# Gate, up and mixer projections that move a fully normalised activation of 384 columns in place of 386 columns with the shift appended

## The chip, the cores and the metric

The kernel runs on one core of a Trainium2 chip, in one launch. The metric is the device time of the whole program in microseconds: the median of several runs. A profile of one execution gives the trace from which all rows below are taken.

## The reference

One inference step through four layers, on 384 tokens (128 context tokens, group 0, and 256 latent tokens, group 1) of width 1024. Layers 0 and 3 mix tokens by latent attention, layer 1 by a gated linear recurrence over eight heads, layer 2 by windowed attention; each layer ends in a SwiGLU FFN of width 2816. Ahead of each mixer and FFN the activation is normalised and modulated, with a scale and a shift that differ by token group:

```python
def _modulate(x, g, shift, scale):
    return _rmsnorm(x, g) * (1.0 + scale) + shift

def _swiglu(h, w_gate, w_up, w_down):
    return (jax.nn.silu(h @ w_gate) * (h @ w_up)) @ w_down

# the recurrent mixer's projections, each 1024 -> 1024
q = heads(jax.nn.silu(xn @ w_q), HG_DK)
v = heads(xn @ w_i, HG_DV)
f_fwd = lb_fwd + (1.0 - lb_fwd) * jax.nn.sigmoid((xn @ w_f[0]).astype(F32))
f_bwd = lb_bwd + (1.0 - lb_bwd) * jax.nn.sigmoid((xn @ w_f[1]).astype(F32))
g = jax.nn.silu((xn @ w_g).reshape(B, S, HG_HEADS, HG_DV).astype(F32))

# per layer
x = x + g1 * mixer(_modulate(x, norm_mix[i], sh1, sc1))
x = x + g2 * _swiglu(_modulate(x, norm_ffn[i], sh2, sc2), ffn_w_gate[i], ffn_w_up[i], ffn_w_down[i])
```

## The kernel before

The activation lies transposed in SBUF as `xT`, eight chunks of 128 features by 384 tokens. A product with a weight is done in blocks of 128 output features. For each block SP loads 128x1024 numbers into one of four `raw` buffers, ACT rounds them into `whi` (L139), and DVE takes the remainder into `wlo` (L140); there are three buffers of each. The activation is split in the same way into `hh` and `hl`. A block is then 24 matmuls, three for each of eight chunks: hi by hi (L146), hi by lo (L147), lo by hi (L148), all added up in one PSUM bank.

The class `Norm` prepares the activation without waiting for the sum of squares. As each residual chunk is written, `chunk` scales it by `A` (gain times one plus scale) into `hh` and `hl`, and adds up its squares. `shift` writes the two shift vectors (one per token group) into two more columns, 384 and 385, of each chunk. `done` reduces the squares with a matmul on PE (L160), takes the reciprocal root on ACT and DVE (`rst`, `rsy`, `rh`: L163 to L167). `proj` runs a block over 386 columns; the last two columns of its result are the projected shift, copied by DVE into `hb` (L361). `scaled` multiplies the other 384 by `rh` into `ev` (L366). The users add `hb` per token group, in two pieces of 128 and 256 tokens: the Silu on ACT and the product on DVE in the FFN, Sigmoid and products in the recurrent mixer. So the first blocks can run while `rh` is still being made.

In an FFN, gate and up blocks alternate, 22 of each; a gate block uses a PSUM tile `acc` (two buffers), an up block `scps` (three). The product is split into `oh`/`ol` (first eight chunks) and `ah`/`al` for the down projection. In the recurrent layer 40 blocks are projected, four pairs of heads by five kinds, in between the steps of the recurrence of the pair before.

Besides, DVE makes the modulation vectors of coming layers: for one in some weight splits it runs two passes named `apr` over a 128x1024 tile (L274). The order on each engine is set by the tile scheduler that builds the program; each engine runs its instructions strictly in that order.

Of the kernel before, what the change touches and what calls it, by code (L numbers as in the profile page):

```python
# [75 lines left out]
def _build(nc, tc, ia, oa, layers, top):  # L76
# [236 lines left out]
    class Norm:  # L313
        def __init__(self, L, which, split=False):
            need(L, 3 * which + 1)
            self.L, self.which = L, which
            self.A = tp.tile([P, 8, 2], F32, tag="modA", name="modA")
            if not split:
                self.scale(0, 8)
            self.hh = hp.tile([P, KD, TB], F32R, tag="hh", name="hh")  # L320
            self.hl = hp.tile([P, KD, TB], F32R, tag="hl", name="hl")
            self.ss = SumSq("x", KD)

        def scale(self, k0, k1):
            L, which = self.L, self.which
# [19 lines left out]
        def done(self):  # L345
            self.r = rstd_of(self.ss.parts, 1024, tp.tile([P, T], F32, tag="rh", name="rh", bufs=1))

        def proj(self, src, pool, mid=None):
            if early:
                ps, b = early.pop(0)  # L350
                return self.scaled(ps), b
            w = wsplit(src, 1024)
            ps = pool()
            if mid:
                gemm(ps[:, :TB], w, 4, self.hh, self.hl, stop=False)
                mid()
# [493 lines left out]
    def hgrn(L, H):  # L850
        with ExitStack() as es:
# [12 lines left out]
            def head_proj(hpair, i, e, D):  # L864
                h = 2 * hpair + e
                if e == 0:
# [7 lines left out]
                    elif i == 4:  # L874
                        D["v"] = p1.tile([P, 3, 256], F32, tag="v", name="hv")
                t, hb = H.proj(ia["hw"][i, h], acc)
                if ev:
                    dst, tv = ev.pop(0)
                    to_tokens(dst, tv, ttp)
                if i == 4:  # L880
                    addb(V, t, t, hb)
                    ev[0] = (D["v"][:, :, e * 128:(e + 1) * 128], t)
                    return
                sg = p2.tile([P, T], F32, tag="sg", name="sg", bufs=1)
                for vv, c0, c1 in GROUPS:
                    last_silu[0] = S.activation(out=sg[:, c0:c1], in_=t[:, c0:c1], func=AF.Sigmoid,
                                                bias=hb[:, vv:vv + 1])
                if i in (0, 3):
                    for vv, c0, c1 in GROUPS:
                        V.scalar_tensor_tensor(out=D["q" if i == 0 else "g"][:, e, c0:c1], in0=t[:, c0:c1],  # L890
                                               scalar=hb[:, vv:vv + 1], in1=sg[:, c0:c1],
                                               op0=ALU.add, op1=ALU.mult)
# [170 lines left out]
    def ffn(L, H, make_next):  # L1063
        with ExitStack() as es:
# [5 lines left out]
            al = p1.tile([P, NFF - KD, T], F32R, name="al")  # L1070
            for f in range(NFF):
                tg, bg = H.proj(ia["gu"][L, f, 0], acc)
                tu, bu = H.proj(ia["gu"][L, f, 1], scp)
                s = p2.tile([P, T], F32, tag="s", name="s")
                for v, c0, c1 in GROUPS:
                    last_silu[0] = S.activation(out=s[:, c0:c1], in_=tg[:, c0:c1], func=AF.Silu, bias=bg[:, v:v + 1])
                for v, c0, c1 in GROUPS:
                    V.scalar_tensor_tensor(out=s[:, c0:c1], in0=tu[:, c0:c1], scalar=bu[:, v:v + 1],
                                           in1=s[:, c0:c1], op0=ALU.add, op1=ALU.mult)
# [241 lines left out]
```

## Time and profile before

| | |
|---|---|
| three runs | 1935.99, 1936.65, 1937.23 us (median 1936.65) |
| profiled execution | 1938.45 us, span of its instructions 1936.7 us |
| granted TensorE clock, mean | 0.996 of full speed |
| PE busy | 1899.5 us, 98 % |
| PEld (weight loads) busy | 1812.3 us, 94 % |
| DVE busy | 1556.3 us, 80 % |
| ACT busy | 873.5 us, 45 % |
| POOL busy | 44.4 us, 2 % |
| DMA | 313.44 MB, mean 162 GB/s |

Busy time counts each stretch in which at least one instruction of the engine is under way. Matmuls are pipelined: each lasts longer than the step from its start to the next one's, so a busy PE says that it never stood still, not how fast it went.

### The profile page before, as it was taken

The numbers are of one execution on the slowest core, as the hardware profiler recorded it, in microseconds if no ns is written. First come the engines' busy times: TensorE is split into PE (matmuls) and PEld (weight loads), VectorE is DVE, ScalarE is ACT, GpSimd is POOL, SyncE is SP. The second block draws the span as 40 slices with busy tenths as digits, with TensorE's granted clock in tenths as the row PEclk, the third lists the DMA queues.
The fourth block names the chain that finished last, engine by engine and source line by source line (L and its number), as shares of the span: only waits on it lengthen the run. The fifth ranks groups of instructions, "written<-read, shape, count | busy, mean of one in ns | idle before, by whom it ended". The sixth has DMA issues, their size and how long they took to land.

```text
span 1936.7 us, 29416 instructions
## 1 busy us (share of the span) xinstructions
PE 1899.5 (98%) x10939; PEld 1812.3 (94%) x10939; DVE 1556.3 (80%) x3097; ACT 873.5 (45%) x1622; POOL 44.4 (2%) x52
## 2 busy tenths in 40 slices
PE   8999999999999999999999999999999999999997
PEld 5768999999999999999999878999999889999997
DVE  3867898888999999898878988989878897755533
ACT  4534534333554554433433675443434555433332
POOL 0000000000011100000000100000000000000000
PEclk9999999999999999999999999999999999999999
DMA  8553566667533334566667423666667334443342
GB/s 331 169 158 112 183 190 208 201 196 207 167 109 100 109 99 125 189 193 207 194 202 228 132 63 123 211 202 199 195 209 213 107 104 142 131 127 124 119 126 71
DMA packets 99343, 313.44 MB, mean 162 GB/s; under 512 B 11008, under 2 KB 20736, under 8 KB 99200
## 3 DMA queue, kind: packets, MB, share of 16 engines
q1 hardware_dynamic: 98768, 310.78, 51.0%
q8 instruction: 86, 1.41, 0.3%
q10 hardware_dynamic: 432, 0.79, 0.1%
q14 instruction: 57, 0.47, 0.1%
HBM read 305.95 MB, written 3.21 MB: 160 GB/s over the span
## 4 chain that ended last, share of the span: by engine, by line
PE 93%; DVE 3%; DMA 2%; ACT 1%; issue 1%; SPq 0%; DVEq 0%; ACTq 0%
PE acc L146 16%; PE acc L147 16%; PE acc L148 16%; PE scps L146 11%; PE scps L147 11%; PE scps L148 11%; PE scps L916 2%; PE misps L506 2%; PE ttps L245 1%; DMA araw<-ada 1%; PE ttps L495 1%; PE ttps L226 1%; DVE apr L274 1%; PE ttps L499 1%; PE misps L160 1%
## 5 line engine op out<-in xcount | busy, mean ns | idle before, releaser
L139 ACT ACTIVATE whi<-raw 128x1024 fp32r<-128x1024 f32 (+1 forms) x381 | 396.6, 1042 | 687.9 <-PE acc L147 327.2
L140 DVE TENSOR_TENSOR wlo<-raw,whi 128x1024 fp32r<-128x1024 f32 x380 | 455.9, 1201 | 109.2 <-ACT whi L139 105.4
L146 PE MATMUL acc<-hh,whi 128*128 128x386 f32 (+1 forms) x1160 | 398.6, 344 | 0.0
L147 PE MATMUL acc<-hl,whi 128*128 128x386 f32 (+1 forms) x1160 | 395.8, 341 | 0.0
L148 PE MATMUL acc<-hh,wlo 128*128 128x386 f32 (+1 forms) x1160 | 393.5, 339 | 0.0
L274 DVE SCALAR_TENSOR_TENSOR apr<-araw,cbc 128x1024 f32<-128x1024 f32 x320 | 390.2, 1219 | 1.8
L146 PE MATMUL scps<-hh,whi 128*128 128x386 f32 (+1 forms) x776 | 264.7, 341 | 0.8 <-ACT hh L341 0.8
L147 PE MATMUL scps<-hl,whi 128*128 128x386 f32 (+1 forms) x776 | 263.5, 340 | 0.3
L148 PE MATMUL scps<-hh,wlo 128*128 128x386 f32 (+1 forms) x776 | 262.4, 338 | 0.0
L146 PEld LDWEIGHTS acc<-hh,whi 128*128 128x128 f32 x1160 | 218.9, 189 | 2.0 <-issue 1.8
L147 PEld LDWEIGHTS acc<-hl,whi 128*128 128x128 f32 x1160 | 219.7, 189 | 0.9
L148 PEld LDWEIGHTS acc<-hh,wlo 128*128 128x128 f32 x1160 | 218.8, 189 | 1.6 <-issue 0.4
L146 PEld LDWEIGHTS scps<-hh,whi 128*128 128x128 f32 x776 | 146.2, 188 | 5.2 <-issue 1.7
L147 PEld LDWEIGHTS scps<-hl,whi 128*128 128x128 f32 x776 | 147.0, 189 | 1.4 <-DVE hl L342 1.1
L148 PEld LDWEIGHTS scps<-hh,wlo 128*128 128x128 f32 x776 | 146.4, 189 | 0.8 <-issue 0.8
L146 PE MATMUL acc<-oh,whi 128*128 128x384 f32 x344 | 118.6, 347 | 7.4 <-DVE xT L387 1.9
L147 PE MATMUL acc<-ol,whi 128*128 128x384 f32 x344 | 118.0, 343 | 0.0
L148 PE MATMUL acc<-oh,wlo 128*128 128x384 f32 x344 | 117.7, 342 | 0.0
L366 DVE TENSOR_TENSOR ev<-acc,rh 128x384 f32<-128x384 f32 x145 | 79.5, 548 | 0.1
L146 PEld LDWEIGHTS acc<-oh,whi 128*128 128x128 f32 x344 | 64.8, 190 | 11.4 <-issue 5.2
L146 PE MATMUL scps<-ah,whi 128*128 128x384 f32 x224 | 75.3, 336 | 0.0
L146 PE MATMUL acc<-ah,whi 128*128 128x384 f32 x224 | 75.3, 336 | 0.0
(309 smaller groups left out, 3196.1 us busy)
## 6 DMA issues: line engine op xcount, KB each, us to landing
raw<-gu SPq DMA_DIRECT2D x176, 512.0 KB, 4.1
araw<-adaT SPq DMA_DIRECT2D x160, 512.0 KB, 3.7
raw<-dn SPq DMA_DIRECT2D x64, 512.0 KB, 4.1
raw<-hw SPq DMA_DIRECT2D x40, 512.0 KB, 3.7
raw<-dn SPq DMA_DIRECT2D x32, 384.0 KB, 3.2
stg<-ada SPq DMA_DIRECT2D x16, 512.0 KB, 6.6
araw<-ada SPq DMA_DIRECT2D x16, 512.0 KB, 4.2
raw<-mo SPq DMA_DIRECT2D x16, 512.0 KB, 3.8
```

The costliest lines, as they stand in the source:

```text
L139: a = S.activation(out=hi[:, :cols], in_=raw[:, :cols], func=AF.Copy)
L140: b = eng.tensor_tensor(out=lo[:, :cols], in0=raw[:, :cols], in1=hi[:, :cols].bitcast(F32), op=ALU.subtract)
L146: TE.matmul(out, lhsT=ah, rhs=bh, start=start, stop=False)
L147: TE.matmul(out, lhsT=ah, rhs=bl, start=False, stop=False)
L148: TE.matmul(out, lhsT=al, rhs=bh, start=False, stop=stop)
L160: TE.matmul(ps, lhsT=ones[n], rhs=q, start=i == 0, stop=i == len(sumsq) - 1)
L226: TE.matmul(ps[32 * q:32 * q + 32, :], lhsT=cond[:, k, :], rhs=raw[:, k2 * 512:(k2 + 1) * 512], start=k < 4, stop=k >= 4, tile_position=(0 ...
L245: TE.matmul(ps[32 * ct:32 * ct + 32, :], lhsT=cond[:, k, :], rhs=raw[:, c2 * 512:(c2 + 1) * 512], start=k == 0, stop=k == 7, tile_position ...
L274: V.scalar_tensor_tensor(out=pr, in0=raw, scalar=1.0, in1=cbc[:, v], op0=ALU.mult, op1=ALU.mult, accum_out=mod_of(L)[:, seg, k, v:v + 1])
L366: V.tensor_tensor(out=t, in0=ps[:, :T], in1=self.r, op=ALU.mult)
L506: TE.matmul(out[:, 128:384], lhsT=v[:, 1 + j, c0:c1], rhs=pt[:, 128 + 256 * j:384 + 256 * j], start=j == 0, stop=j == 2, **kw)
L916: TE.matmul(ps[:, tt], lhsT=Lt[:, e, tt], rhs=rhs(e, t), start=True, stop=True)
```

## The change

In FFNs and in the recurrent mixer the first block runs as before, over 386 columns. The next three run side by side (`group`): for each chunk, three matmuls of each of the three blocks into three PSUM tiles, and then that chunk is rewritten in place by `whole`: `xT` times `rh` on DVE (`hx`), scale and shift on ACT in two pieces, rounding into `hh` on ACT, remainder into `hl` on DVE. All later blocks read 384 columns of the rewritten chunks, and their result is used straight from PSUM, without `hb` and `ev`. The third weight of a group is split into a spare tile: `ah`/`al` in the FFN, which is not in use yet. Attention mixers keep the old form.

```diff
+        def whole(self, k):
+            h = tp.tile([P, T], F32, tag="sq", name="hx")
+            B = mods[self.L][:, 3 * self.which, k]
+            V.tensor_tensor(out=h, in0=xT[:, k], in1=self.r, op=ALU.mult)
+            for v, c0, c1 in GROUPS:
+                S.activation(out=h[:, c0:c1], in_=h[:, c0:c1], func=AF.Identity, scale=self.A[:, k, v:v + 1],
+                             bias=B[:, v:v + 1])
+            S.activation(out=self.hh[:, k, 0:T], in_=h, func=AF.Copy)
+            V.tensor_tensor(out=self.hl[:, k, 0:T], in0=h, in1=self.hh[:, k, 0:T].bitcast(F32), op=ALU.subtract)
+
+        def group(self, blocks):
+            ws = [wsplit(src, 1024, into=into) for src, _, into in blocks]
+            pss = [pool() for _, pool, _ in blocks]
+            for k in range(KD):
+                for (hi, lo), ps in zip(ws, pss):
+                    c = slice(k * 128, k * 128 + 128)
+                    mm3(ps[:, :TB], hi[:, c], lo[:, c], self.hh[:, k], self.hl[:, k], k == 0, k == KD - 1)
+                self.whole(k)
+            self.begun.extend(pss)
+            self.full = True
+
         def proj(self, src, pool, mid=None):
...
+            if self.begun:
+                ps = self.begun.pop(0)
+                b = tp.tile([P, 2], F32, tag="hb", name="hb", bufs=8)
+                V.tensor_copy(out=b, in_=ps[:, T:TB])
+                return self.scaled(ps), b
             w = wsplit(src, 1024)
             ps = pool()
+            if self.full:
+                gemm(ps[:, :T], w, 8, self.hh[:, :, 0:T], self.hl[:, :, 0:T])
+                return ps[:, :T], None
...
                 t, hb = H.proj(ia["hw"][i, h], acc)
+                if not H.full:
+                    H.group([(ia["hw"][1, h + 1], scp, None), (ia["hw"][2, h], acc, None),
+                             (ia["hw"][2, h + 1], scp, spare2())])
...
                 tg, bg = H.proj(ia["gu"][L, f, 0], acc)
+                if f == 0:
+                    spare = [x.rearrange("p f t -> p (f t)")[:, 0:1024] for x in (ah, al)]
+                    H.group([(ia["gu"][L, 0, 1], scp, None), (ia["gu"][L, 1, 0], acc, None),
+                             (ia["gu"][L, 1, 1], scp, spare)])
                 tu, bu = H.proj(ia["gu"][L, f, 1], scp)
                 s = p2.tile([P, T], F32, tag="s", name="s")
...
+                if bg is None:
+                    last_silu[0] = S.activation(out=s, in_=tg, func=AF.Silu)
+                    V.tensor_tensor(out=s, in0=tu, in1=s, op=ALU.mult)
```

First place: DVE in layer 0's FFN. Before, where the third to fifth blocks are evicted (numbers tell buffers apart; L361 is the bias copy, L366 the multiplication by `rh`, L1078 the product's halves, L1082 the remainder of the product, L140 a weight split):

```order
L361 COPY hb_2158<-acc_2133 128x2
L366 TENSOR_TENSOR ev_2160<-acc_2133,rh_2026 128x384
L274 SCALAR_TENSOR_TENSOR apr_2212,mod_113<-araw_2089,cbc_93 128x1024
L140 TENSOR_TENSOR wlo_2247<-raw_2244,whi_2246 128x1024
L361 COPY hb_2195<-scps_2170 128x2
L366 TENSOR_TENSOR ev_2197<-scps_2170,rh_2026 128x384
L1078 SCALAR_TENSOR_TENSOR s_2199<-ev_2197,hb_2195,s_2199 128x128
L1078 SCALAR_TENSOR_TENSOR s_2199<-ev_2197,hb_2195,s_2199 128x256
```

After the change, the evictions of the three grouped blocks stand among the rewrites (L353 is `hx`, L358 the new `hl`; L378 and L397 copy the bias and multiply by `rh`). Directly ahead of these rows stand the bias copy and the multiplication of the first grouped block, `scps_2103`, and ahead of those the rewrites of chunks 0 to 2 and the `hx` of chunks 3 and 4:

```order
L378 COPY hb_2237<-acc_2104 128x2
L1121 SCALAR_TENSOR_TENSOR s_2230<-ev_2228,hb_2226,s_2230 128x128
L1121 SCALAR_TENSOR_TENSOR s_2230<-ev_2228,hb_2226,s_2230 128x256
L358 TENSOR_TENSOR hl_1785<-hx_2160,hh_1784 128x384
L397 TENSOR_TENSOR ev_2239<-acc_2104,rh_2026 128x384
L353 TENSOR_TENSOR hx_2190<-xT_78,rh_2026 128x384
L1125 TENSOR_TENSOR ol_2045<-s_2230,oh_2044 128x384
L358 TENSOR_TENSOR hl_1785<-hx_2175,hh_1784 128x384
L378 COPY hb_2241<-scps_2105 128x2
L353 TENSOR_TENSOR hx_2205<-xT_78,rh_2026 128x384
L397 TENSOR_TENSOR ev_2243<-scps_2105,rh_2026 128x384
L140 TENSOR_TENSOR wlo_2289<-raw_2286,whi_2288 128x1024
```

The `hl` of chunks 3 and 4 and the split for the sixth block now stand behind evictions of grouped blocks, which end together.

Second place: PE behind the group in the same FFN. Before, blocks followed each other whole (here the end of the fourth and the start of the fifth; L146 to L148 as above):

```order
L146 MATMUL scps_2170<-hh_1784,whi_2164 128x386
L147 MATMUL scps_2170<-hl_1785,whi_2164 128x386
L148 MATMUL scps_2170<-hh_1784,wlo_2165 128x386
L146 MATMUL acc_2215<-hh_1784,whi_2208 128x386
L147 MATMUL acc_2215<-hl_1785,whi_2208 128x386
L148 MATMUL acc_2215<-hh_1784,wlo_2209 128x386
```

After, the fifth block (`acc_2261`) has done four chunks when the sixth (`scps_2294`) is woven in; the rows are the 13th to the 20th behind the group:

```order
L146 MATMUL acc_2261<-hh_1784,whi_2254 128x384
L146 MATMUL scps_2294<-hh_1784,whi_2288 128x384
L147 MATMUL scps_2294<-hl_1785,whi_2288 128x384
L147 MATMUL acc_2261<-hl_1785,whi_2254 128x384
L148 MATMUL acc_2261<-hh_1784,wlo_2255 128x384
L146 MATMUL acc_2261<-hh_1784,whi_2254 128x384
L148 MATMUL scps_2294<-hh_1784,wlo_2289 128x384
L146 MATMUL scps_2294<-hh_1784,whi_2288 128x384
```

The first matmul that reads `wlo_2289` has 18 matmuls ahead of it since the group's end; the `hl` of the last chunk is read after 39. In layer 1's FFN these counts are 15 and 45, in layer 2's 18 and 46, in layer 3's as in layer 0's; in the recurrent layer the fifth block runs whole, and the last `hl` is read after 22.

Third place: DVE in layer 2's FFN, from the first step of the reciprocal root. Before:

```order
L165 SCALAR_TENSOR_TENSOR rst_12238<-misps_12235,rsy_12237 128x384
L361 COPY hb_12290<-acc_12265 128x2
L166 SCALAR_TENSOR_TENSOR rst_12238<-rst_12238,rsy_12237 128x384
L274 SCALAR_TENSOR_TENSOR apr_12344,mod_8438<-araw_12191,cbc_93 128x1024
L167 SCALAR_TENSOR_TENSOR rh_12234<-rst_12238,rsy_12237 128x384
L274 SCALAR_TENSOR_TENSOR apr_12344,mod_8438<-araw_12191,cbc_93 128x1024
L366 TENSOR_TENSOR ev_12292<-acc_12265,rh_12234 128x384
L361 COPY hb_12327<-scps_12302 128x2
L366 TENSOR_TENSOR ev_12329<-scps_12302,rh_12234 128x384
L140 TENSOR_TENSOR wlo_12381<-raw_12378,whi_12380 128x1024
```

After:

```order
L165 SCALAR_TENSOR_TENSOR rst_11790<-misps_11787,rsy_11789 128x384
L392 COPY hb_11842<-acc_11817 128x2
L166 SCALAR_TENSOR_TENSOR rst_11790<-rst_11790,rsy_11789 128x384
L274 SCALAR_TENSOR_TENSOR apr_11860,mod_8136<-araw_11743,cbc_93 128x1024
L167 SCALAR_TENSOR_TENSOR rh_11786<-rst_11790,rsy_11789 128x384
L274 SCALAR_TENSOR_TENSOR apr_11860,mod_8136<-araw_11743,cbc_93 128x1024
L397 TENSOR_TENSOR ev_11844<-acc_11817,rh_11786 128x384
L140 TENSOR_TENSOR al_11807<-raw_11865,ah_11806 128x1024
L353 TENSOR_TENSOR hx_11881<-xT_78,rh_11786 128x384
L353 TENSOR_TENSOR hx_11896<-xT_78,rh_11786 128x384
L140 TENSOR_TENSOR wlo_12021<-raw_12018,whi_12020 128x1024
L274 SCALAR_TENSOR_TENSOR apr_12024,mod_8136<-araw_11852,cbc_93 128x1024
```

The split of the group's third weight (`al`) now stands behind `rh`, and the first `hl` comes after it, another split and a further `apr`. From the first of these rows to the `hl` of chunk 7 there are 42 in all: 25 of 384 columns, six `apr`, three splits, two pairs of halves and four bias copies. In the recurrent layer the same stretch has 46: 25 of 384 columns, two splits, two `apr`, four bias copies and 13 small ones.

## Rows read from the trace of the kernel before

**Rows 1.** The page, part 1: busy us (share of the span) xinstructions by engine.

```profile
PE 1899.5 (98%) x10939; PEld 1812.3 (94%) x10939; DVE 1556.3 (80%) x3097; ACT 873.5 (45%) x1622; POOL 44.4 (2%) x52
```

**Rows 2.** Busy time by stretch: us, PE, PEld, DVE, ACT, POOL, clock, DMA, GB/s.

```profile
217.00:403.00 186.00, 186.00 (x1055) 185.87 (x1054) 162.94 (x305) 77.22 (x114) 0.00 (x0) 1.00 0.63 194
495.00:782.00 287.00, 282.78 (x1802) 277.10 (x1801) 267.98 (x576) 150.28 (x326) 25.86 (x23) 1.00 0.36 114
```

**Rows 3.** Timeline of PE, matmuls of three widths: start, duration, line, operation.

```profile
222.96 0.34 PE L146 MATMUL acc<-hh,whi 128*128 128x386 f32 x1
...
231.43 0.34 PE L146 MATMUL acc<-hh,whi 128*128 128x386 f32 x1
...
420.12 0.34 PE L146 MATMUL scps<-ah,whi 128*128 128x384 f32 x1
...
423.76 0.33 PE L146 MATMUL acc<-oh,whi 128*128 128x384 f32 x1
...
427.97 0.34 PE L146 MATMUL acc<-ah,whi 128*128 128x384 f32 x1
...
33.68 0.34 PE L147 MATMUL scps<-hl,whi 128*128 128x384 f32 x1
...
35.60 0.34 PE L146 MATMUL scps<-hh,whi 128*128 128x384 f32 x1
...
1518.04 0.39 PE L612 MATMUL acc<-whi,ch 128*128 128x512 f32 x1
...
1519.20 0.40 PE L614 MATMUL acc<-whi,cl 128*128 128x512 f32 x1
```

**Rows 4.** Weight loads by line and form: count, busy us, mean ns, idle before.

```profile
L147 PEld LDWEIGHTS acc<-hl,whi 128*128 128x128 f32 x1160 | 219.7, 189 | 0.9
```

**Rows 5.** Timeline of DVE in layer 0's FFN, 232 to 236 us.

```profile
232.37 0.75 DVE L1078 SCALAR_TENSOR_TENSOR s<-ev,hb,s 128x128 f32<-128x128 f32 x2
233.04 1.22 DVE L140 TENSOR_TENSOR wlo<-raw,whi 128x1024 fp32r<-128x1024 f32 x1
234.17 0.55 DVE L1082 TENSOR_TENSOR ol<-s,oh 128x384 fp32r<-128x384 f32 x1
234.64 1.22 DVE L274 SCALAR_TENSOR_TENSOR apr<-araw,cbc 128x1024 f32<-128x1024 f32 x1
235.79 0.08 DVE L274 DVE_READ_ACCUMULATOR apr<-araw,cbc 128x1 f32 x1
235.86 0.16 DVE L361 COPY hb<-acc 128x2 f32<-128x2 f32 x1
235.94 0.55 DVE L366 TENSOR_TENSOR ev<-acc,rh 128x384 f32<-128x384 f32 x1
```

**Rows 6.** ACT operations by line and form: count, busy us, mean ns, idle before.

```profile
L139 ACT ACTIVATE whi<-raw 128x1024 fp32r<-128x1024 f32 x349 | 369.5, 1060 | 626.6 <-PE acc L147 296.8 <-issue 242.5 <-PE scps L147 85.2
L341 ACT ACTIVATE hh<-xT,modA 128x256 fp32r<-128x256 f32 x64 | 31.7, 496 | 0.0
L1081 ACT ACTIVATE ah<-s 128x384 fp32r<-128x384 f32 x56 | 29.5, 526 | 72.8 <-DVE s L1078 72.8
L341 ACT ACTIVATE hh<-xT,modA 128x128 fp32r<-128x128 f32 x64 | 24.9, 389 | 2.8 <-DVE xT L387 1.6 <-DVE modA L327 1.0
```

**Rows 7.** Timeline of PE: first matmul of the fifth block in layers 1, 2.

```profile
796.29 0.34 PE L146 MATMUL acc<-hh,whi 128*128 128x386 f32 x1
...
1225.62 0.34 PE L146 MATMUL acc<-hh,whi 128*128 128x386 f32 x1
```

**Rows 8.** Timeline of DVE: recurrent layer, and the root in layer 2's FFN.

```profile
497.92 0.55 DVE L165 SCALAR_TENSOR_TENSOR rst<-misps,rsy 128x384 f32<-128x384 f32 x1
...
510.77 0.16 DVE L361 COPY hb<-acc 128x2 f32<-128x2 f32 x1 [0.70 <-PE acc L148]
...
1213.45 0.55 DVE L165 SCALAR_TENSOR_TENSOR rst<-misps,rsy 128x384 f32<-128x384 f32 x1
```

**Rows 9.** Timeline of DVE: a remainder that waits for ACT's rounding.

```profile
337.24 0.56 DVE L1082 TENSOR_TENSOR al<-s,ah 128x384 fp32r<-128x384 f32 x1 [0.29 <-ACT ah L1081]
```

More of the change, by code (lines that the diff above doesn't have):

```diff
@@ L322, in __init__ @@
             self.ss = SumSq("x", KD)
+            self.begun = []
+            self.full = False
         def scale(self, k0, k1):
@@ L880, in head_proj @@
                 if i == 4:
-                    addb(V, t, t, hb)
-                    ev[0] = (D["v"][:, :, e * 128:(e + 1) * 128], t)
+                    tv = tp.tile([P, T], F32, tag="ev", name="ev", bufs=3)
+                    V.tensor_copy(out=tv, in_=t)
+                    ev[0] = (D["v"][:, :, e * 128:(e + 1) * 128], tv)
                     return
                 sg = p2.tile([P, T], F32, tag="sg", name="sg", bufs=1)
-                for vv, c0, c1 in GROUPS:
-                    last_silu[0] = S.activation(out=sg[:, c0:c1], in_=t[:, c0:c1], func=AF.Sigmoid,
-                                                bias=hb[:, vv:vv + 1])
+                if hb is None:
+                    last_silu[0] = S.activation(out=sg, in_=t, func=AF.Sigmoid)
+                else:
+                    for vv, c0, c1 in GROUPS:
+                        last_silu[0] = S.activation(out=sg[:, c0:c1], in_=t[:, c0:c1], func=AF.Sigmoid,
+                                                    bias=hb[:, vv:vv + 1])
                 if i in (0, 3):
[L889 to L892, printed above, removed]
+                    V.tensor_tensor(out=D["q" if i == 0 else "g"][:, e], in0=t, in1=sg, op=ALU.mult)
                 else:
@@ L1072, in ffn @@
                 tg, bg = H.proj(ia["gu"][L, f, 0], acc)
+                if f == 0:
+                    spare = [x.rearrange("p f t -> p (f t)")[:, 0:1024] for x in (ah, al)]
+                    H.group([(ia["gu"][L, 0, 1], scp, None), (ia["gu"][L, 1, 0], acc, None),
+                             (ia["gu"][L, 1, 1], scp, spare)])
                 tu, bu = H.proj(ia["gu"][L, f, 1], scp)
                 s = p2.tile([P, T], F32, tag="s", name="s")
[L1075 to L1079, printed above, removed]
+                if bg is None:
+                    last_silu[0] = S.activation(out=s, in_=tg, func=AF.Silu)
+                    V.tensor_tensor(out=s, in0=tu, in1=s, op=ALU.mult)
+                else:
+                    for v, c0, c1 in GROUPS:
+                        last_silu[0] = S.activation(out=s[:, c0:c1], in_=tg[:, c0:c1], func=AF.Silu, bias=bg[:, v:v + 1])
+                    for v, c0, c1 in GROUPS:
+                        V.scalar_tensor_tensor(out=s[:, c0:c1], in0=tu[:, c0:c1], scalar=bu[:, v:v + 1],
+                                               in1=s[:, c0:c1], op0=ALU.add, op1=ALU.mult)
                 dh, dl = (bh[:, f], bl[:, f]) if f < KD else (ah[:, f - KD], al[:, f - KD])
```

## Prediction

> **What bounds the kernel now.** I read the page's busy shares first: PE has work in flight for 1899.5 of 1936.7 us [rows 1]. Then busy time by stretch. In the 186 us of gate and up blocks of layer 0's FFN, matmuls and weight loads are both solid, DVE is busy 162.9 us and ACT 77.2; the recurrent layer (495 to 782 us) leaves PE idle only 4.2 of 287 us, with DVE busy 268 [rows 2]. So in the stretches that the change touches PE sets the time, and it has no stall to give back. What can move the end is the time from one matmul to the next, and any new wait of PE. DVE is second, at 88 to 93 per cent. For prices I then read the timelines, since the duration of a row is no price: matmuls overlap, and a DVE row starts before the one ahead has ended. Steps from start to start count.
>
> **Narrower matmuls.** By the two listings, 4704 matmuls go from 386 to 384 columns: 40 blocks of 24 in each of four FFNs, 36 of 24 in the recurrent layer. Two whole 386 blocks take 222.96 to 231.43, 48 steps of 176.5 ns. At 384 columns the steps are 173.3 ns from `ah` (21 steps, 420.12 to 423.76), 175.4 from `oh` (24 steps, 423.76 to 427.97), and 174.5 from `hh` itself in the first layer's early blocks (11 steps, 33.68 to 35.60) [rows 3]. That is 1.1 to 3.2 ns less for each. The rows on `hh` are the nearest, but they are few and stand in another stage; between them (2.0) and `oh` (1.1) I take 1.5 ns: 4704 x 1.5 = 7.1 us gained. The bounds are 4.2 us (below) and 4704 x 3.2 = 15 us.
>
> Is the step set by columns at all? 512 columns take 232 ns (five steps, 1518.04 to 1519.20) and 384 some 174, with the same 128x128 weight load of 189 ns in front [rows 3, 4]: 58 ns for 128 columns, 0.45 ns a column, so two columns are worth 0.9 ns, or 4.2 us over all. The Trainium skill ("TensorE: Matmul & The Clock Gate", Back-to-back issue gap) says that in a stream of load and matmul pairs both set the spacing. By it, with loads as solid as they are here, the narrowing could be worth nothing; the 512-column rows speak against that.
>
> **Work that goes.** Of the later blocks, the bias copies, the multiplications by `rh` and one of each pair of halves go from DVE. With the steps of [rows 5] (0.08 for a copy, 0.47 for a 384-wide tensor operation, 0.67 for a pair of halves) that is some 1.3 us of DVE per gate and up pair. It lies beside matmuls throughout: PE has no wait there for it to shorten, so I cost it at nothing. In the recurrent layer it could return part of the 4.2 us of PE idle time; I take zero and keep 4.2 as a bound.
>
> **Work that comes, and where.** Each rewrite of a chunk is two DVE operations of 384 (0.47 each) and on ACT two Identity pieces and a Copy, by the nearest rows 0.39, 0.50 and 0.53 us long [rows 6], about 1.1 us by steps. Eight chunks are 7.5 us of DVE and 9 of ACT. The cover is the group: 72 matmuls, 12.7 us of PE. But chunk k may only be rewritten when the group's three blocks have read it, nothing can start before `rh`, and both engines still have their old work. So I add up what stands on DVE.
>
> *FFN of layer 0.* In the listing, the bias copy of the first grouped block (`hb<-scps`) stands ahead of the `hl` of chunks 3 to 7, so it cannot start until that block's last matmul, seven from the group's end: 231.43 - 7 x 0.1765 + 0.34 = 230.53. From it to the end of the split that the next up block needs (`wlo`) stand three small copies (0.3 with their latency), two halves (0.67), eight operations of 384 (3.8) and the split (1.22): 6.0 us, so 236.5. PE reaches the first matmul on that `wlo` after 18 others, at 231.43 + 18 x 0.175 = 234.6 [rows 3, 5]. PE waits **1.9 us**. The order in layer 3's FFN is the same: **1.9 us**.
>
> *FFN of layer 1.* The same chain of 6.0 us starts 0.86 before the group's end at 796.29 [rows 7]; the `wlo` is wanted after 15 matmuls: 801.4 against 798.9, **2.5 us**.
>
> *FFN of layer 2.* Here the sums for the next layer's modulation (`apr`, 1.22 us a step) lie thickest. From the first `rst` at 1213.45 [rows 8] to the last `hl` DVE has 25 operations of 384 (11.75), six `apr` (7.3), three splits (3.4), two pairs of halves (1.3) and four copies (0.4): 24.3 us with the last one's full length, so 1237.7. PE wants it after 46 matmuls from 1225.62 [rows 7], at 1233.7: **4.1 us**, spread over several chunks.
>
> *Recurrent layer.* The copies of blocks 2 to 4 follow their last matmuls, the third at 510.77 [rows 8]; so the group ends at 510.77 - 0.03 - 0.34 + 0.18 = 510.6. From `rst` at 497.92 DVE has 25 operations of 384 (11.75, the two forget gates taken alike), two splits (2.3), two `apr` (2.4), four copies (0.4) and 13 small ones (1.3): 18.3 us, so 516.2. In this order nothing of another block fills the gap: the last `hl` is wanted after 22 matmuls, at 514.4. That is 1.8 us, and with the next block's split behind it 0.5 more: **2.3 us**.
>
> The five come to 12.7 us. These sums leave out the waits of DVE for ACT and back; one such hand-over shows 0.29 us of idle DVE [rows 9]. At one for each place I add 1.5: 14.2 us. If each of eight chunks paid it in each place, it would be 12 us instead. The lower bound is half the 12.7, since later matmuls of other blocks could use part of each wait.
>
> **Sum.** 14.2 - 7.1 = +7.1 us. The profiled execution took 1938.45 us (span 1936.7), so its like would take 1945.6; the median of the runs is 1.8 us lower than that execution, hence 1936.65 + 7.1 = **1943.8 us**. A difference under 0.2 per cent (3.9 us) can't be told from none.
>
> **Rivals.**
> *The rewriting is hidden, and the kernel is faster.* If PE never meets a late chunk, only the columns count: 1929.6, or 1922 with the 3.2 ns of the `ah` rows. For it: ACT is busy under half of the stretch [rows 2]. Against it: the chain of 6.0 us that starts after the first grouped block has finished, whatever ACT does. It decides when that chain is under some 4 us.
>
> *A draw.* Waits of 7 us and 7 us of columns, or 12.7 against the full 15. Time about 1936.
>
> *Weight loads set the pace.* Nothing from the columns: 1936.65 + 14.2 = 1951. For it: loads without a gap [rows 2]; against it: the steps of [rows 3].
>
> *A wait ahead of the group.* The group's third weight is split early into the spare tile, ahead of the chunks of the last residual on ACT; where its load has not landed, ACT stops, the sum of squares comes late, and the reduction that stands inside block 1 on PE with it. One split is 1.22 on DVE and 1.06 on ACT; if it delays PE once at each of five places it is 5 us more: 1949.
>
> *The narrowing doesn't show.* The chunks of `hh` keep their 386-column stride; if the start of a chunk and not its width makes `hh` slower than `ah` (176.5 against 173.3), the lower bound of 4.2 us holds, and the time is 1946.7; that lies within the forecast's own case.
>
> **Chances.** Waits exceed the columns, by 4 to 13 us: 0.58. Loads set the pace: 0.04. The wait ahead of the group adds its 5 us: 0.05. All three are slower. Draw: 0.20. Hidden and faster: 0.13. So slower 0.67, same 0.20, faster 0.13. Waits between 6.4 and 25 us and columns between 4.2 and 15 give extremes of -9 and +20; leaving out the far ends of both, one in ten on each side, gives 1933 to 1952. The forecast's own case runs from 1940.5 to 1950.
>
> **What the new profile would show.** Right: later gate and up blocks step at about 175 ns, with no bias copies and no multiplications by `rh` between them; PE idle times after each of the five groups, released by DVE (`wlo`, `hl`) or ACT (`hh`), of 2 to 4 us in all, most in layer 2; DVE busy about 137 us (162.9 less 20 pairs of 1.3) in the 186 us of FFN. Wrong: PE solid through the blocks behind the groups; or 386 and 384 columns at one step; or a stall in block 1, ahead of the group. It would be wrong above all if PE's order lets other matmuls run through each wait, or if the steps at 384 columns come out at 173.

## The result, and the profile after the change

| | before | after |
|---|---|---|
| median of the runs | 1936.43 us (1935.99 to 1937.23, 4 runs) | 1950.77 us (1949.61 to 1951.14, 4 runs) |
| ratio, with its 95 % interval | | 1.0074 (1.0061 to 1.0087) |
| span of the profiled execution | 1936.7 us | 1949.3 us |

The change made the kernel 14.3 us slower. The forecast said slower (0.67), 1943.8 us, 1933 to 1952: the side and the range held, the size was half of what came.

The page of the changed kernel, part 1, answers to [rows 1]:

```profile
PE 1906.9 (98%) x10939; PEld 1810.9 (93%) x10939; DVE 1464.5 (75%) x2681; ACT 883.4 (45%) x1634; POOL 44.3 (2%) x52
```

DVE lost 92 us of work and PE gained 7 us of busy time with the same count of matmuls: the work taken off bought nothing in the FFNs, and 1.8 us in the recurrent layer (shown in the part on the prediction). The first view to read is what PE waited for (us in total, times, the longest); before, only the last kind was there, with 0.6 us:

```profile
PE acc L146 <- ACT hh L357: 3.9, 8, 0.6
...
PE scps L148 <- DVE wlo L140: 1.6, 3, 0.5
...
PE acc L147 <- DVE hl L358: 1.2, 5, 0.4
...
PE acc L148 <- DVE wlo L140: 0.8, 2, 0.6
```

They are idle time alone, 7.5 us with the 0.6 of before among them, and less than the loss. The steps from one matmul's start to the next tell more. The table takes each stretch from the first matmul of one reduction (L160) to that of the next. "Waits" is what its steps over 230 ns hold beyond 175 ns, steps of 310 to 330 ns set apart, both less the same in the trace of before; the reduction's own first step is left out.

| stretch | before, us | after, us | difference | waits | steps of 320 ns |
|---|---|---|---|---|---|
| FFN, layer 0 | 278.64 | 279.70 | +1.06 | 2.11 | 0 |
| recurrent layer | 286.98 | 291.43 | +4.45 | 2.72 | 2.16 (15 more) |
| FFN, layer 1 | 278.30 | 280.92 | +2.62 | 3.68 | 0 |
| FFN, layer 2 | 279.52 | 284.85 | +5.33 | 4.31 | 2.03 (14) |
| FFN, layer 3 | 276.18 | 277.25 | +1.07 | 2.12 | 0 |

Waits are 14.9 us and the steps of 320 ns 4.2; the five differences are 14.5, so 4.6 us came back, which wide and norewrite below put down to the columns. (Ahead of the first stretch the changed kernel was 1.6 us earlier in this execution; in the profiles of the kernels that leave that part as it was, the stretch starts anywhere from 215.0 to 216.6 us. The mixers of layers 2 and 3 differ by -0.3 and +0.2.)

In the recurrent layer the last two columns are net figures. Behind the group alone the waits hold 4.8 us, and 13 steps of 320 ns 1.9; in the rest of the layer the two together come to 1.8 less than before. In the FFNs nearly all lies behind the group. So the five groups cost 17.0 us of waits (0.2 of them ahead of layer 2's), and 27 steps of 320 ns 3.9.

**A wait that came as worked out.** Layer 0's FFN, DVE and PE, from the timelines:

```profile
228.98 0.16 DVE L378 COPY hb<-scps 128x2 f32<-128x2 f32 x1 [1.18 <-PE scps L148]
...
233.72 1.21 DVE L140 TENSOR_TENSOR wlo<-raw,whi 128x1024 fp32r<-128x1024 f32 x1
...
234.03 0.44 PE L146 MATMUL acc<-hh,whi 128*128 128x384 f32 x1 [0.61 <-ACT hh L357]
234.99 0.44 PE L148 MATMUL scps<-hh,wlo 128*128 128x384 f32 x1 [0.52 <-DVE wlo L140]
235.26 0.34 PE L146 MATMUL scps<-hh,whi 128*128 128x384 f32 x1
```

The bias copy waits for the first grouped block, and the split that PE needs ends at 234.93. The forecast had 230.53 and 236.5 on the clock of before, 228.96 and 234.93 with the 1.57 us that this stretch began earlier. Each wait also costs more than its idle time: the step behind it is 0.27 to 0.29 us in place of 0.175.

**What was not in the forecast.** In the recurrent layer, PE's busy time (count), granted clock, DMA share and GB/s by stretches of 1 us:

```profile
511.00:512.00 1.00, 1.00 (x8) 1.00 0.25 98
...
513.00:514.00 1.00, 0.55 (x2) 1.00 0.00 0
514.00:515.00 1.00, 0.51 (x2) 1.00 0.00 0
515.00:516.00 1.00, 0.76 (x3) 1.00 0.00 0
516.00:517.00 1.00, 0.64 (x3) 0.91 0.00 0
517.00:518.00 1.00, 0.99 (x3) 0.50 0.00 0
...
522.00:523.00 1.00, 1.00 (x5) 0.50 0.75 131
523.00:524.00 1.00, 1.00 (x6) 0.68 0.51 201
524.00:525.00 1.00, 1.00 (x7) 1.00 0.71 291
```

and PE's timeline there:

```profile
515.09 0.44 PE L146 MATMUL acc<-hh,whi 128*128 128x384 f32 x1 [0.59 <-ACT hh L357]
...
516.67 0.59 PE L146 MATMUL acc<-hh,whi 128*128 128x384 f32 x1 [0.36 <-ACT hh L357]
...
521.05 0.53 PE L147 MATMUL acc<-hl,whi 128*128 128x384 f32 x1
521.37 0.53 PE L148 MATMUL acc<-hh,wlo 128*128 128x384 f32 x1
521.69 0.53 PE L146 MATMUL acc<-hh,whi 128*128 128x384 f32 x1
```

From 513 on PE stands still by turns, never over 0.6 us at a time. At some 517 the granted clock goes from full to 0.50, which is 1.2 GHz, and stays there until 523.7; the last matmul that waits starts at 519.3. In that time a step is 320 ns in place of 175: a matmul that waits for nobody costs 0.145 us more. In layer 2's FFN the same lasts from 1237 to 1244. The Trainium skill ("TensorE: Matmul & The Clock Gate", A second HAM failure mode: psum-queue depth-cycling) tells of short idle times of PE between groups of matmuls that are enough to throttle the clock; the trace agrees.

### The profile page after: what moved, and what is told of

It is laid out like the page before. It is cut to its first block, busy times and chain, and to the rows that moved or that the text cites. A ratio compares the mean times of both kernels' runs of the same rounds, so it can differ in the third digit from the quotient of the medians.

```text
span 1949.3 us, 29058 instructions
## 1 busy us (share of the span) xinstructions
PE 1906.9 (98%) x10939; PEld 1810.9 (93%) x10939; DVE 1464.5 (75%) x2681; ACT 883.4 (45%) x1634; POOL 44.3 (2%) x52
## 4 chain that ended last, share of the span: by engine, by line
PE 91%; DVE 4%; ACT 2%; DMA 2%; issue 1%; SPq 0%; DVEq 0%; ACTq 0%
PE acc L146 16%; PE acc L148 16%; PE acc L147 16%; PE scps L148 11%; PE scps L147 11%; PE scps L146 11%; PE scps L951 2%; PE misps L537 2%; PE ttps L245 1%; DMA araw<-ada 1%; PE ttps L526 1%; PE ttps L226 1%; PE ttps L530 1%; PE misps L160 1%; DVE apr L274 1%
## 5 line engine op out<-in xcount | busy, mean ns | idle before, releaser
L139 ACT ACTIVATE whi<-raw 128x1024 fp32r<-128x1024 f32 (+1 forms) x376 | 391.3, 1042 | 793.6 <-issue 374.8
L140 DVE TENSOR_TENSOR wlo<-raw,whi 128x1024 fp32r<-128x1024 f32 (+1 forms) x375 | 449.4, 1199 | 221.0 <-ACT whi L139 213.5
L146 PE MATMUL acc<-hh,whi 128*128 128x384 f32 (+1 forms) x1144 | 393.6, 344 | 4.1 <-ACT hh L357 3.9
L147 PE MATMUL acc<-hl,whi 128*128 128x384 f32 (+1 forms) x1144 | 392.3, 343 | 1.3 <-DVE hl L358 1.2
L148 PE MATMUL acc<-hh,wlo 128*128 128x384 f32 (+1 forms) x1144 | 390.0, 341 | 0.3 <-DVE wlo L140 0.3
L148 PE MATMUL scps<-hh,wlo 128*128 128x384 f32 (+1 forms) x752 | 255.7, 340 | 1.6 <-DVE wlo L140 1.6
L146 PE MATMUL scps<-hh,whi 128*128 128x384 f32 (+1 forms) x752 | 254.7, 339 | 1.2 <-ACT hh L343 0.8
L147 PE MATMUL scps<-hl,whi 128*128 128x384 f32 (+1 forms) x752 | 255.4, 340 | 0.3
L146 PEld LDWEIGHTS acc<-hh,whi 128*128 128x128 f32 x1144 | 217.1, 190 | 10.9 <-ACT hh L357 8.5
L147 PEld LDWEIGHTS acc<-hl,whi 128*128 128x128 f32 x1144 | 216.3, 189 | 5.1 <-DVE hl L358 4.0
L148 PEld LDWEIGHTS acc<-hh,wlo 128*128 128x128 f32 x1144 | 217.1, 190 | 2.5 <-DVE wlo L140 0.9
L146 PEld LDWEIGHTS scps<-hh,whi 128*128 128x128 f32 x752 | 142.4, 189 | 5.1 <-issue 1.7
L148 PEld LDWEIGHTS scps<-hh,wlo 128*128 128x128 f32 x752 | 142.6, 190 | 3.2 <-DVE wlo L140 2.3
L147 PEld LDWEIGHTS scps<-hl,whi 128*128 128x128 f32 x752 | 141.8, 189 | 1.4 <-DVE hl L344 1.1
L146 PE MATMUL acc<-oh,whi 128*128 128x384 f32 x344 | 118.7, 347 | 5.9 <-DVE xT L418 1.9
L147 PE MATMUL acc<-ol,whi 128*128 128x384 f32 x344 | 117.8, 342 | 0.0
L148 PE MATMUL acc<-oh,wlo 128*128 128x384 f32 x344 | 117.6, 342 | 0.0
L1116 DVE TENSOR_TENSOR s<-scps,s 128x384 f32<-128x384 f32 x80 | 44.4, 555 | 82.2 <-PE scps L148 82.2
L146 PE MATMUL acc<-ah,whi 128*128 128x384 f32 x224 | 75.3, 336 | 0.0
L146 PE MATMUL scps<-ah,whi 128*128 128x384 f32 x224 | 75.3, 336 | 0.0
L147 PE MATMUL acc<-al,whi 128*128 128x384 f32 x224 | 75.3, 336 | 0.0
```

Of the source, the lines that this page charges most:

```text
L139: a = S.activation(out=hi[:, :cols], in_=raw[:, :cols], func=AF.Copy)
L140: b = eng.tensor_tensor(out=lo[:, :cols], in0=raw[:, :cols], in1=hi[:, :cols].bitcast(F32), op=ALU.subtract)
L146: TE.matmul(out, lhsT=ah, rhs=bh, start=start, stop=False)
L147: TE.matmul(out, lhsT=ah, rhs=bl, start=False, stop=False)
L148: TE.matmul(out, lhsT=al, rhs=bh, start=False, stop=stop)
L1116: V.tensor_tensor(out=s, in0=tu, in1=s, op=ALU.mult)
```

## Experiments

Each was timed in five rounds against the kernel before, which stood at 1936.1 to 1936.3 us. All differences below, of a stretch or a median, are to the kernel before unless said otherwise. Differences of whole profiled spans hold one thing that no edit made: in layer 3's mixer the traces of before, of the changed kernel and of pool have 16 to 19 steps of 320 ns, those of all others 5 to 8, three among them, which leaves this mixer as it was. That is 1.2 to 2 us of such a span. By stretch (as in the table above; FFNs by their layer):

| kernel | median, us | FFN 0 | recurrent | FFN 1 | FFN 2 | FFN 3 |
|---|---|---|---|---|---|---|
| changed | 1950.77 | +1.06 | +4.45 | +2.62 | +5.33 | +1.07 |
| wide | 1954.27 | +2.07 | +4.55 | +4.65 | +5.09 | +2.08 |
| fill | 1947.09 | +1.05 | +2.58 | +2.61 | +3.74 | +1.11 |
| three | 1942.17 | +1.10 | -0.03 | +2.61 | +0.00 | +1.09 |
| norewrite | 1931.49 | -1.09 | -0.62 | -1.13 | -0.74 | -1.06 |
| pool | 1962.39 | +5.02 | +6.04 | +4.14 | +6.45 | +6.34 |
| hx8 | 1947.59 | +0.92 | +1.31 | +3.84 | +4.67 | +0.95 |
| hold | 1939.57 | +0.72 | +1.32 | +1.25 | +0.47 | +0.75 |
| hx8_hold | 1936.31 | +0.14 | +0.55 | +0.43 | -0.12 | +0.18 |
| ffn_hx8_hold | 1938.06 | +0.16 | -0.62 | +0.44 | -0.07 | +0.18 |

### What the columns are worth: wide, norewrite

```diff
 wide
-                gemm(ps[:, :T], w, 8, self.hh[:, :, 0:T], self.hl[:, :, 0:T])
+                gemm(ps[:, :TB], w, 8, self.hh, self.hl)
 norewrite
-                self.whole(k)
...
-                return ps[:, :T], None
+                return self.scaled(ps), self.hb
```

> The changed kernel, but the later blocks move all 386 columns again (their last two results are not used). Forecast's price of 1.5 ns for each of 4704 matmuls: 7.1 us slower than the changed kernel, about 1957.9. By the steps in the new trace (24 matmuls of a later FFN block 4.208 us against 4.233, in the recurrent layer 4.291 against 4.305): 160 x 0.026 + 36 x 0.014 = 4.7 us slower, about 1955.5. If width counts for nothing: 1950.8, with steps still at 4.208 us per block.

> The changed kernel without the rewriting: chunks stay as they were, later blocks move 384 columns and are multiplied by rh at their eviction as before; their shift is left out (the first one's stands in for it). Theory that the loss is the rewriting's waits and the clock that falls on them, and that the narrowing gives 26 ns a block in the FFNs and 14 in the recurrent layer: no wait behind the groups, no step of 320 ns there, 1936.4 - 4.7 = 1931.7. By the forecast's 1.5 ns a matmul: 1929.3. If running three blocks side by side or the early third split costs by itself: 1934 or more.

wide: ratio 1.0092 (1.0079 to 1.0106), 3.5 us over the changed kernel by the medians, where 4.7 were expected. In layers 0 and 3, where no clock fell in either, the stretch grew by exactly 1.01 us, 40 blocks of 0.025. The other places mix in a clock that fell in layer 1's FFN (10 steps of 320 ns, none before) and for a shorter time in layer 2's. norewrite: 1931.49, ratio 0.9978 (0.9969 to 0.9987), against 1931.7 expected. PE is solid behind the groups, at full clock, and the FFNs are 0.7 to 1.1 us shorter. So the grouping and the early third split cost next to nothing (0.3 us of waits in layer 2's FFN); the loss is the rewriting, and the most that this narrowing can give by itself is 4.7 us. PE behind the group in the recurrent layer (the columns are PE's busy time, count, granted clock, DMA share and GB/s):

```profile
511.00:517.00 6.00, 6.00 (x36) 1.00 0.71 192
```

The steps themselves, two whole blocks later on in the changed kernel (48 steps of 175.2 ns), and in wide (176.25):

```profile
303.49 0.33 PE L146 MATMUL scps<-hh,whi 128*128 128x384 f32 x1
...
311.90 0.33 PE L146 MATMUL scps<-hh,whi 128*128 128x384 f32 x1
```

```profile
304.31 0.34 PE L146 MATMUL scps<-hh,whi 128*128 128x386 f32 x1
...
312.77 0.34 PE L146 MATMUL scps<-hh,whi 128*128 128x386 f32 x1
```

### Whether the clock fell on PE's standstill: fill, three

```diff
 fill: in the first block behind the group, two places, FILL = (0, 0, 4, 4, 4, 4, 4, 4)
+                    for k in range(KD):
+                        mm3(ps[:, :T], ..., self.hh[:, k, 0:T], self.hl[:, k, 0:T], k == 0, k == KD - 1)
+                        for _ in range(FILL[k]):
+                            TE.matmul(junk[:, :T], lhsT=w[0][:, 0:128], rhs=self.hh[:, 0, 0:T], ...)
 three: the recurrent layer in its old form, and
-                if f == 0:
+                if f == 0 and L != 2:
```

> The changed kernel, with 48 matmuls more, whose results nobody reads, in the fifth block of the recurrent layer and of layer 2's FFN: they read a chunk that is already rewritten, and stand on PE between the chunks that come late. If PE's own standstill is what the clock fell on: no steps of 320 ns in these two places, the granted clock stays at 1.0 there, 4.4 us less than the changed kernel (about 1946.4), or up to 2 us less good where a chunk comes in time and the added matmuls (48 x 0.175 = 8.4 us in all, against some 8 us of waits) hold PE up. If the 320 ns came from DVE and ACT at work on the same memory, which the filling does not change: the steps stay at 320 ns, and the time rises by up to 8 us. If the waits alone made the loss: no gain.

> The change in the FFNs of layers 0, 1 and 3 alone; the recurrent layer and layer 2's FFN as before. Theory that the loss lies in two places (between the reductions, +4.45 us in the recurrent layer and +5.33 in layer 2's FFN): 1950.8 - 9.8 = 1941.0, which is still 4.5 us above the kernel before, with layers 0 and 3 at +1.1 and layer 1 at +2.6, and no step of 320 ns behind a group. Rival: the loss is spread, or it comes from the scheduler's changed order elsewhere: over 1944. If the two places are all of it: 1936.

fill: 1947.09, ratio 1.0058 (1.0045 to 1.0071), 3.7 us under the changed kernel where 4.4 were expected. In the recurrent layer, the same columns as above:

```profile
513.00:514.00 1.00, 1.00 (x8) 1.00 0.03 8
...
516.00:517.00 1.00, 1.00 (x8) 1.00 0.00 0
...
520.00:521.00 1.00, 0.71 (x4) 1.00 0.00 0
521.00:522.00 1.00, 1.00 (x8) 1.00 0.68 70
```

PE does useless work for about as long as it would have waited, DVE and ACT do what they did (8.24 and 9.87 us busy in the ten from 511, against 8.24 and 10.00 in the changed kernel's ten from 510), and the clock stays at full. The 24 added matmuls of each place take 4.2 us; the waits behind the group fell from 4.8 to 0.5 us in the recurrent layer and from 4.3 to 0.5 in layer 2's FFN. The 1.87 and 1.59 us won by place are the half clock less what the filling held up. So PE's own standstill brought the clock down: the work of DVE and ACT on the same memory was the same as before, and the 320 ns are gone.

three: 1942.17, ratio 1.0029 (1.0018 to 1.004), 1941.0 expected. The three stretches that keep the change stand at +1.10, +2.61 and +1.09 and the two others at 0: each place pays for itself.

### Where the waits come from: pool, hx8, hold

```diff
 pool
-            V.tensor_tensor(out=h, in0=xT[:, k], in1=self.r, op=ALU.mult)
+            G.tensor_tensor(out=h, in0=xT[:, k], in1=self.r, op=ALU.mult)
 hx8: a place of its own for each chunk's hx (FFN: al's memory, al itself taken at f == 8)
-            h = tp.tile([P, T], F32, tag="sq", name="hx")
...
-                self.whole(k)
+                self.whole(k, hx[k])
 hold: FEED = 0.66, HOLD = 6
     def ada_tick(d, a, b):
+        if hold[0]:
+            return
...
         def done(self):
+            hold[0] = self.which == 1
...
         def proj(self, src, pool, mid=None):
+            if self.full:
+                self.n += 1
+                if self.n > HOLD:
+                    hold[0] = False
```

> The changed kernel with the first step of a rewrite (hx, xT times rh) on POOL in place of DVE. Eight of 0.47 us leave DVE in each place, POOL takes some 1.3 us for one. If DVE's queue makes the waits, as forecast: FFNs of layers 0 and 3: the chain of 6.0 us loses 5 x 0.47 = 2.35, no wait (1.9 less each); layer 1 2.3 less, layer 2 3.8 less; the recurrent layer up to 2 less, with the clock at full speed in layer 2's FFN: 11 to 14 us less, 1937 to 1940. If ACT is what comes last (PE's waits for hh are 3.9 us of those behind the groups), with five ACT operations and more between hx and hl: under 3 us less, 1948 or more. If POOL is too slow for two chunks at a time: slower than 1951.

> The changed kernel with a place of its own for the hx of each of the eight chunks (in al's memory in the FFN, in K2's and Q2's in the recurrent layer), in place of two places that take turns. The work is the same. Theory of the two places (the third hx can't start before the first hl is done, so a rewrite's five steps run nearly one behind the other): most of the 15 us of waits goes, and with it the half clock, 1936 to 1941. Theory of the forecast, that the sum of DVE's work behind rh makes the waits: the same sum, 1947 to 1951, with PE waiting for the same splits.

> The changed kernel, where no apr is issued from an FFN's reduction on until three more blocks behind the group have been split, and a little more often later (0.66 for each split in place of 0.6). Forecast's sums: in layer 2's FFN six apr of 1.22 us go from the stretch, more than the wait of 4.1, so no wait and no half clock there: 5 to 6 us; in layers 0 and 3 no apr stands in the chain of 6.0 us, nothing; layer 1 up to 1; recurrent layer the same: together 1944 to 1945. Theory of the two places for hx: layer 2's FFN then waits like layers 0 and 3, 2 us, with no half clock: 1946 to 1948.

pool went the other way, 1962.39, ratio 1.0135 (1.0122 to 1.0149). DVE and POOL in layer 0's FFN:

```profile
225.85 0.56 DVE L358 TENSOR_TENSOR hl<-hx,hh 128x384 fp32r<-128x384 f32 x1 [1.91 <-ACT hh L357]
228.47 0.56 DVE L358 TENSOR_TENSOR hl<-hx,hh 128x384 fp32r<-128x384 f32 x1 [2.06 <-ACT hh L357]
```

```profile
226.49 1.02 POOL L353 TENSOR_TENSOR hx<-xT,rh 128x384 f32<-128x384 f32 x1 [1.68 <-DVE hl L358]
229.12 1.01 POOL L353 TENSOR_TENSOR hx<-xT,rh 128x384 f32<-128x384 f32 x1 [1.60 <-DVE hl L358]
```

DVE now idles 2 us before an `hl` and POOL 1.6 us before an `hx`: with two places for `hx`, a slower first step makes a ring of POOL, ACT and DVE that goes round once for two chunks. This is read from the rows; pool with eight places was not run. It suggested that the ring binds in the changed kernel too, and hx8 was made to test it. The ring fell in the FFNs as they stand: hx8 is 1947.59 (ratio 1.0057, 1.0044 to 1.0069), its FFNs of layers 0, 2 and 3 better by 0.1 to 0.7 us alone, layer 1 worse by 1.2, where now the clock fell. In the recurrent layer it held in part, 3.1 us better: the waits behind the group fell from 4.8 to 3.5 us, and no step there is one of 320 ns (13 in the changed kernel).

hold is the strong one: 1939.57, ratio 1.0015 (1.0006 to 1.0024), 11.2 us under the changed kernel (13 by the profiled spans), where the forecast's sums gave 6 to 7. The four FFNs give 6.9: layer 2's 4.86, where those sums had 5 to 6 and no wait left, and layer 1's 1.37; in layers 0 and 3, whose chain holds no `apr`, 0.3 each. The other part I did not expect: 3.1 in the recurrent layer, which has three `apr` between its reduction and the last `hl` in both kernels, and 3 in the attention mixers. Of the 3.1 only about 1 lies behind the group, where the waits are the same 4.8 us and 7 steps in place of 13 ran at half clock; 2 lie in the rest of the layer, where among others a wait of PE of 1.5 us for an `hh` at the layer's end is gone. Of the 3 in the mixers 1.9 lie in layer 3's, whose steps at half clock three lacks too, without any edit there. There the order moved with the feed; how that led to these gains I did not trace. Layer 2's FFN in hold, DVE and PE (L389 is the bias copy here, L141 the split, L147 and L149 are L146 and L148 of the changed kernel):

```profile
1224.99 0.16 DVE L389 COPY hb<-scps 128x2 f32<-128x2 f32 x1 [0.75 <-PE scps L149]
...
1229.72 1.22 DVE L141 TENSOR_TENSOR wlo<-raw,whi 128x1024 fp32r<-128x1024 f32 x1
```

```profile
1230.03 0.44 PE L147 MATMUL acc<-hh,whi 128*128 128x384 f32 x1 [0.55 <-ACT hh L364]
1230.99 0.45 PE L149 MATMUL scps<-hh,wlo 128*128 128x384 f32 x1 [0.53 <-DVE wlo L141]
```

With the `apr` gone, what stays is layer 0's chain: the same 5.95 us from the bias copy to the end of the split, and a wait of 1.7 us, as in layer 0 (1.8). That layer 2 would then wait like layers 0 and 3 is what the theory of the two places had named.

### Both, and the FFNs alone: hx8_hold, ffn_hx8_hold

> Both: eight places for hx, and no apr in the stretch. By the forecast's sums only the second counts: 1944. By the two places the first counts in all five groups: 1934 to 1938. If neither: 1950.

> As the last, in the FFNs alone (the recurrent layer as before the change; apr held two blocks longer, 0.7 for each split). If the four FFNs then wait for nothing: 160 blocks x 0.026 = 4.2 us less than the kernel before, 1932. If each keeps its 2 us: 1940. If only layers 0 and 3 keep theirs: 1936.

hx8_hold: 1936.31, ratio 1.0003 (0.9994 to 1.0011), no difference from the kernel before. That lies where the theory of the two places had put it (1934 to 1938), and not at the 1944 of the forecast's sums: on top of hold the eight places take another 0.6 to 0.8 us out of each of the five stretches, and no step behind a group ran at half clock. In the FFNs the narrowing's 4.2 us (160 blocks of 0.026) are there and are paid back by the split that is still late in every one (steps over 230 ns hold 1.2 us each beyond those of before). ffn_hx8_hold: 1938.06, ratio 1.0007 (0.9998 to 1.0016): its FFNs do the same, and layer 2's mixer lost 2.2 us that the last kernel had not, 0.8 of it in steps of 320 ns; I did not trace what set that off. No kernel here that computes the whole beats the one before.

### Where a chunk starts: pad400, after_pad400

```diff
-            self.hh = hp.tile([P, KD, TB], F32R, tag="hh", name="hh")
+            self.hh = hp.tile([P, KD, 400], F32R, tag="hh", name="hh")[:, :, 0:TB]
```

(and so for `hl`, in the kernel before and in the changed one; pool_pad400 has this and the edit of pool)

> The kernel before, with the chunks of hh and hl 400 columns apart (1600 bytes) in place of 386; still 386 columns are moved, and the order on all engines is the same. If where a chunk starts makes the steps on hh slower than those on ah (4.233 us per block against 4.157 to 4.169): with the two columns at 0.45 ns each, some 4.18, that is 196 blocks and more x 0.05 = 10 us less, about 1926. If it starts don't matter: 1936.4, and the steps keep their 4.233. In between, if only every second chunk gains: about 1931.

> The changed kernel with the chunks of hh and hl 400 columns (1600 bytes) apart, order unchanged. With 386 columns that stride gave 4.252 us a block in place of 4.233, so a start on 64 bytes alone does not help. If start and length together must be whole multiples of 64 bytes, as with ah (4.157 to 4.169): blocks of 4.16 to 4.17, 160 x 0.043 + 36 x 0.02 = 7.6 us less than the changed kernel, about 1943. If the place in memory that sets it is another: 4.20 to 4.25, 1950 to 1958.

> Both edits in one. If each does what it does alone, the sum of the two gains: 1930 to 1933 where both succeed, which would be under the kernel before; 1943 where only the stride does, 1937 to 1940 where only POOL does.

The gain that each of the three looked for did not come; after_pad400 landed where its last rival had put it. pad400: 1938.06, ratio 1.0009 (1.0 to 1.0017), blocks of 4.252 us in place of 4.233; after_pad400: 1951.71, ratio 1.0083 (1.0069 to 1.0096), 4.226 in place of 4.208; pool_pad400: 1964.35, ratio 1.0139 (1.0123 to 1.0154). Two columns are worth 0.025 to 0.026 us a block at either distance, so the distance of 386 hides nothing of the narrowing. But the padding also moved `oh`, by 896 bytes if tiles lie in the order in which they are made (8 chunks of 14 columns of 4 bytes more in `hh` and as many in `hl`), and there, in a tile that no edit touched, 24 steps fell from 4.21 us [rows 3] to 4.17 in pad400:

```profile
425.25 0.34 PE L146 MATMUL acc<-oh,whi 128*128 128x384 f32 x1
...
429.42 0.33 PE L146 MATMUL acc<-ah,whi 128*128 128x384 f32 x1
```

What in the place of a tile makes such a difference stays open.

## Why the prediction was right, and where it was off

**Waits behind the groups: right in kind, their sum near by luck in part.** 14.2 us were forecast, and 14.9 is the net figure of the table; behind the groups themselves it is 17.0. Layers 0 and 3: 1.9 each without hand-overs, 2.1; layer 1: 2.5 and 3.7, of which 0.8 is a wait at 812.4 for a later block's `whi`, which no term had; layer 2: 4.1 and 4.3, with the last `hl` done at 1244.2 where 1237.7 plus the 6.2 us of delay up to there gives 1243.9; the recurrent layer: 2.3 and 4.8, the longest, where layer 2 had been named. Where it was short, ACT was late and not DVE: in the recurrent layer DVE idles ahead of the last two `hl`,

```profile
515.07 0.56 DVE L358 TENSOR_TENSOR hl<-hx,hh 128x384 fp32r<-128x384 f32 x1 [0.30 <-ACT hh L357]
516.65 0.56 DVE L358 TENSOR_TENSOR hl<-hx,hh 128x384 fp32r<-128x384 f32 x1 [1.02 <-ACT hh L357]
```

since sigmoids and forget gates stand between the steps of a rewrite on ACT. That DVE's work behind `rh` makes waits in the FFNs was shown by hold for the `apr`: without them layer 2's FFN waits 1.7 us in place of 4.3 and layer 1's 2.0 in place of 3.7. The ring of the two places counts for 0.6 to 0.8 us in each stretch on top of hold. For the rest the cause is argued and not shown: the chain on DVE fits in order and length, but in layer 0 ACT waits 1.31 us for PE and then works without a gap as well, and the first of PE's two long waits there is put down to its `hh`. No run took work off ACT alone.

```profile
228.81 1.06 ACT L139 ACTIVATE whi<-raw 128x1024 fp32r<-128x1024 f32 x1 [1.31 <-PE scps L147]
```

**The missing term: the clock.** The sum took a wait to cost its own length. 3.9 us came on top, in 27 matmuls that waited for nobody, since PE stood still often enough for the granted clock to fall to 1.2 GHz. fill showed the cause. No step of the forecast looked for it, though every wait in it stood on PE among matmuls at full clock.

**The mis-sized term: the columns.** 7.1 us at 1.5 ns a matmul; 4.6 in the trace of the changed kernel, 4.7 in norewrite. The rows on `hh` at 384 columns in layer 0's early blocks, to which I had leaned, were too few and stood elsewhere; the slope from 512 to 384 columns, 0.9 ns for two, was the right row, and had been put down as the lower bound. Together with the term that follows: 7.1 + 2.8 of waits + 3.9 of clock + 2.5 of columns - 1.8 = 14.5.

**The term put at nothing: work that goes.** In the FFNs it gave nothing, as forecast. In the recurrent layer the forecast took zero, with PE's 4.2 us of idle time as a bound, and 1.8 came, from evictions that are shorter on DVE and ACT. From the 180th matmul behind the reduction to the layer's end the changed kernel gained 2.2 us on the one before; wide, which has the shorter evictions and not the narrowing, gained 1.8; norewrite, which has the narrowing and the old evictions, 0.5; three, which has neither there, 0.05. The largest single wait of PE before, and what stands in its place after:

```profile
755.26 0.44 PE L146 MATMUL acc<-oh,whi 128*128 128x384 f32 x1 [1.62 <-ACT oh L1033]
```

```profile
758.80 0.85 PE L1064 MATMUL ttps<-ident,o 128*128 128x128 f32 x3 [0.81 <-ACT o L1060]
```

**DVE's busy time in the FFN.** The answer to [rows 2], the same 186 us of layer 0's FFN:

```profile
215.43:401.43 186.00, 184.87 (x1049) 183.51 (x1048) 144.07 (x220) 78.59 (x118) 0.00 (x0) 1.00 0.63 192
```

144.1 us of DVE; I had written 137 and left out the 7.5 us of the rewriting itself, which falls into the window.

**The range.** That it held is luck in part. The forecast's own case ended at 1950, below the result; three terms missed by 9.2 us to one side, and the work that goes took 1.8 back.

**The rivals.** Hidden and faster, and the draw, fell by the waits. A wait ahead of the group came to 0.2 us in layer 2's FFN, and nowhere else. The narrowing that doesn't show because of the distance fell by pad400 and after_pad400, though its 4.2 us for the columns was near. The rival of the weight loads, by which the columns give nothing, had named 1951, within 0.3 us of the result, and was wrong: wide and norewrite show that the columns do count. A right number is no proof of its mechanism.

## What to carry to other kernels

A stall on TensorE can be priced twice: its own length, and, as in two of the five places here where short ones followed each other closely, the matmuls after it at half clock; read the granted clock in fine stretches behind every new wait. A one-time rewriting that is hidden by its cover on average must still be added up in the order of the engine that does it, with everything that stands in the queue (here six `apr` of 1.22 us) and up to the first consumer, not the last. Work taken off an engine that is not the bottleneck is worth nothing only where PE never waits for it; where PE has some idle time, as in the recurrent layer, count that too. And before paying for a narrowing, measure what a column costs, from rows that differ in width alone: here 0.54 ns, so that 4704 shorter matmuls were worth some 5 us.

## What the runs showed of the hardware that was not expected

The granted clock fell to 0.50 though PE never idled over 0.6 us at a time, and whether it falls is a close thing. With the same order on PE up to that point it fell in layer 1's FFN in wide (10 steps of 320 ns) and not in the changed kernel, on waits of about the same sum (3.3 and 3.7 us). In hx8 it fell there too:

```profile
803.00:805.00 2.00, 1.23 (x4) 1.00 0.00 0
805.00:807.00 2.00, 1.66 (x5) 0.56 0.43 61
807.00:809.00 2.00, 2.00 (x8) 0.59 0.52 201
```

In two traces neither the longest standstill nor the sum decided it. In the recurrent layer of hx8_hold PE stood still for 2.84 us at once, behind the same group, and the granted clock stayed at full; in the changed kernel 1.6 us in pieces of at most 0.59 had gone before it fell:

```profile
511.00:514.00 3.00, 0.39 (x3) 1.00 0.01 3
514.00:520.00 6.00, 5.54 (x30) 1.00 0.32 89
```

```profile
514.23 0.45 PE L149 MATMUL acc<-hh,wlo 128*128 128x384 f32 x1 [2.84 <-DVE wlo L141]
```

The place of a tile in memory changed the steps of its matmuls by 1.6 ns (`oh` in pad400, 175.4 to 173.8), more than two columns do. And moving a step to an idle engine made the kernel 11.6 us slower than the changed one (pool): that engine took 1.02 us in the rows above (1.33 in the mean of 40) where DVE steps by 0.47; that the two places for `hx` turned the difference into waits of all three engines is read from the rows and was not tested.
